# Seven products for eight in the gate, branch and output projections, over one set of PSUM banks

## The chip, the cores and the metric

The kernel runs on one core of a Trainium2 chip. The metric is the device time of one execution in microseconds. Before the change three runs took 2945.49, 2949.14 and 2949.18 us; the median is 2949.14 us.

## What is computed

One layer of a hybrid encoder block over 256 tokens of width 4096, in float32:

```
h    = rms_norm(x)                                    # x: 256 x 4096
proj = h @ w_in                                       # 4096 -> q,k,v,gate, indexer, z,x,B,C,dt, merge logits
y_a  = attention(top 64 keys of an indexer) * silu(gate_a)        # 256 x 2048
y_b  = ssd_mixer(conv, scan) * silu(z), grouped norm              # 256 x 2048
g    = sigmoid(merge logits)                          # two gates of 256 x 4096
out  = (g0 * (y_a @ w_branch_attn) + g1 * (y_b @ w_branch_ssd)) @ w_out
x    = x + rms_norm(out)
```

The change is in the last three lines and in the part of `proj` that gives the merge logits: the gate projection (4096 to 8192 columns), the branch projections (two of 2048 to 4096) and the output projection (4096 to 4096).

## The kernel before

**Three matmuls for one product.** Each float32 operand is split in two parts of a reduced format, high and low: `h = round(a)`, `l = a - h`. A product of a 128 x 128 block of activations (the stationary operand) with a 128 x 512 block of weights is three matmuls into one PSUM bank: low x high, high x low, high x high. ScalarE makes the high part of the weights (L144, L147), VectorE the low part (L145, L148), 1024 elements a row at a time, because two K blocks ("a half") are split together. The activations are split once and stay in SBUF: `xh`, `xl`, then `yah`, `yal` and `ybh`, `ybl` for the branches, `mh`, `ml` for the output projection.

**`gemm`** (L118) does 512 output columns: 32 K blocks (16 in a branch) times two token tiles of 128, so 192 matmuls (96 in a branch), into two banks. The accumulators rotate over two pairs of banks, four more banks are free for other work (`aux_bank`). Weights come in chunks of 1 MB (`raw`, 3 buffers), SyncE issues them. The high and low parts have 3 buffers each (`WBUFS`).

**Side work** runs as generators in a queue `aux`. `step()` advances the first one after each half; `push` adds one. The evacuation of a gemm's two banks is such a generator: it is pushed when the gemm's last matmul has been recorded, and so runs beside the next gemm.

**The stages**: indexer and attention, then the SSD mixer, then a loop over `n` of eight blocks of 512 columns, each with two gate gemms, the attention branch and the SSD branch, then eight output gemms and the final norm. `ev_gate` (L669) takes a sigmoid out of PSUM, `ev_branch` multiplies a branch's PSUM result by it (L678) and GpSimd adds the two branches (L685). The merged block is transposed on TensorE (`transpose4`) and written to DRAM (`mscr`, L699) by GpSimd's DMA queue; `load_merged` (L703 to L712) reads it back near the end and splits it (L709, L710). A scheduler orders the recorded instructions of each engine by their dependencies and their place in the program; each engine then works in order.

Of the kernel before, what the change touches and what calls it, by code (L numbers as in the profile page):

```python
# [22 lines left out]
KC = 4  # L23
HK = 2
WBUFS = 3
EPS = 1e-6
# [4 lines left out]
QSCALE = 128 ** -0.5  # L31
ISCALE = 32 ** -0.5 * 64 ** -0.5
# [6 lines left out]
def fused_block(tc, x, xT, w_qi, w_misc, w_attn, w_ssd, w_gate, w_br, w_out,  # L39
# [13 lines left out]
    dram = root(tc.tile_pool(name="dram", bufs=1, space=bass.MemoryType.DRAM))  # L53

    def aux_bank():
        return paux.tile([P, NW], F32, tag="aux", name="aux")

    xh = big.tile([P, KT, S], F32R, tag="bh", name="xh")
    xl = big.tile([P, KT, S], F32R, tag="bl", name="xl")
# [20 lines left out]
    yraw = [yr.tile([P, 2, S], F32, tag=f"yr{i}", name=f"yraw{i}") for i in range(8)]  # L80

    # ---------------------------------------------------------------- helpers
# [35 lines left out]
    def gemm(chunks, nk, act, evac, prep=None, plan=None, done=None):  # L118
        while len(live) > 1:
            drain(live.popleft())  # L120
        ps = {t: pmain.tile([P, NW], F32, tag=f"acc{t}", name=f"acc{t}") for t in range(2)}
# [44 lines left out]
    def gemm_misc(evac):  # L166
        while len(live) > 1:
            drain(live.popleft())
        ps = pmain.tile([P, S], F32, tag="acc0", name="accm")
        for c in range(KT // KC):  # L170
# [6 lines left out]
            for i in range(KC):  # L177
                k = c * KC + i
                T.matmul(ps, wh[:, i, :], xl[:, k, :], start=(k == 0), stop=False)
                T.matmul(ps, wl[:, i, :], xh[:, k, :], start=False, stop=False)  # L180
                T.matmul(ps, wh[:, i, :], xh[:, k, :], start=False, stop=(k == KT - 1))
# [3 lines left out]
    def xact(k):  # L185
        return xh[:, k, :], xl[:, k, :]

    # ------------------------------------------------------ start: x, its rstd
# [25 lines left out]
    def split_x(k, xk):  # L214
        g = pc[:, PC_GAIN + k:PC_GAIN + k + 1]
        A.activation(xh[:, k, :], xk, AF.Copy, scale=g)
        V.scalar_tensor_tensor(xl[:, k, :], xk, g, xh[:, k, :].bitcast(F32),
                               ALU.mult, ALU.subtract)
# [20 lines left out]
    # ------------------------------------------------------------ attention  # L239
# [26 lines left out]
    def evac_misc(ps):  # L266
# [17 lines left out]
        # softplus(v) = max(v, 0) + log1p(exp(-|v|)), log1p(e) = 2 atanh(e / (2 + e))  # L284
# [93 lines left out]
    def attention_unit(j):  # L378
# [24 lines left out]
        def attend():  # L403
            for t in range(2):
# [46 lines left out]
                for i in range(2):  # L451
                    V.tensor_copy(yraw[2 * j + i][:, :, t * P:(t + 1) * P],
                                  b3[:, 2 * i:2 * i + 2, :])
                yield
# [4 lines left out]
    for j in range(2):  # L459
        gemm([w_qi[j, c] for c in range(8)], KT, xact, qi_rope(j), prep=None if j else prep_x)  # L460
# [3 lines left out]
    for j in range(2, 4):  # L464
        gemm([w_qi[j, c] for c in range(8)], KT, xact, qi_rope(j))
        push(qi_score(j))
    push(topk())
    for j in range(4):
        evs, attend = attention_unit(j)
        for i in range(4):  # L470
            gemm([w_attn[j, i, c] for c in range(8)], KT, xact, evs[i])
        push(attend())

    # ----------------------------------------------------------------- SSD
# [8 lines left out]
    def to_ssd():  # L483
        nonlocal ssdp, ssdp_cm, ybp_cm, ybh, ybl
# [3 lines left out]
        ybp_cm, ybp = open_pool("ybp")  # L488
        ybh = ybp.tile([P, 16, S], F32R, name="ybh")
        ybl = ybp.tile([P, 16, S], F32R, name="ybl")  # L490
        ssdp_cm, ssdp = open_pool("ssdp")

    ssdp = ssdp_cm = ybp_cm = ybh = ybl = None
# [399 lines left out]
```

## Time and profile before

| | |
|---|---|
| time, three runs | 2945.49, 2949.14, 2949.18 us |
| profiled execution, span from first to last instruction | 2946.0 us |
| TensorE busy | 2923.5 us, 13260 matmuls |
| VectorE busy | 1560.6 us |
| ScalarE busy | 1336.8 us |
| GpSimd busy | 198.9 us |
| DMA | 568.09 MB, mean 193 GB/s |

The page gives no other time for the profiled execution than its span, which lies within the three runs. The matmul column counts time in which at least one matmul was in flight; one matmul's row is longer than the distance from its start to the next one's start, since they are pipelined. The same holds for VectorE and ScalarE instructions that stand back to back. Times per stage, distances and waits are in the rows further down.

### The profile page before, as it was taken

The numbers are of one execution on the slowest core, as the hardware profiler recorded it, in microseconds if no ns is written. First come the engines' busy times: TensorE is split into PE (matmuls) and PEld (weight loads), VectorE is DVE, ScalarE is ACT, GpSimd is POOL, SyncE is SP. The second block draws the span as 40 slices with busy tenths as digits, with TensorE's granted clock in tenths as the row PEclk, the third lists the DMA queues.
The fourth block names the chain that finished last, engine by engine and source line by source line (L and its number), as shares of the span: only waits on it lengthen the run. The fifth ranks groups of instructions, "written<-read, shape, count | busy, mean of one in ns | idle before, by whom it ended". The sixth has DMA issues, their size and how long they took to land.

```text
span 2946.0 us, 33033 instructions
## 1 busy us (share of the span) xinstructions
PE 2923.5 (99%) x13260; PEld 2414.2 (82%) x13260; DVE 1560.6 (53%) x1750; ACT 1336.8 (45%) x1548; POOL 198.9 (7%) x150
## 2 busy tenths in 40 slices
PE   9999999999999999999999999999999999999997
PEld 7878888888888888888888888888888888888886
DVE  6677445454454656565655444444444444544445
ACT  6444444444444545555555344444444444444444
POOL 0100000000000103030300000000000000000001
PEclk9999999999999999999999999999999999999998
DMA  9544555545555454545455555555555555675554
GB/s 334 179 168 173 190 181 185 187 171 192 180 186 187 170 184 174 175 168 187 170 186 183 203 194 199 190 203 188 204 195 196 197 192 201 235 269 197 192 194 157
DMA packets 86555, 568.09 MB, mean 193 GB/s; under 512 B 9728, under 2 KB 10496, under 8 KB 20864
## 3 DMA queue, kind: packets, MB, share of 16 engines
q1 hardware_dynamic: 85392, 562.30, 53.7%
q0 software_dynamic: 1008, 3.67, 0.3%
q8 instruction: 104, 1.70, 0.2%
q14 instruction: 51, 0.42, 0.0%
HBM read 558.06 MB, written 7.86 MB: 192 GB/s over the span
## 4 chain that ended last, share of the span: by engine, by line
PE 97%; DMA 1%; DVE 1%; ACT 0%; issue 0%; SPq 0%; ACTq 0%; DVEq 0%
PE acc L156 31%; PE acc L158 31%; PE acc L157 31%; DMA mr<-mscr 1%; PE aux L322 1%; PE aux L581 0%; DMA raw<-w_qi_d 0%; PE aux L350 0%; PE aux L439 0%; PE aux L412 0%; PE aux L571 0%; DVE og L786 0%; PE aux L510 0%; DVE wl L148 0%; PE aux L432 0%
## 5 line engine op out<-in xcount | busy, mean ns | idle before, releaser
L148 DVE TENSOR_TENSOR wl<-raw,wh 128x1024 fp32r<-128x1024 f32 x1011 | 1255.8, 1243 | 1234.8 <-ACT wh L147 1232.6
L147 ACT ACTIVATE wh<-raw 128x1024 fp32r<-128x1024 f32 x1011 | 1071.3, 1060 | 1477.0 <-PE acc L158 1437.6
L156 PE MATMUL acc<-wh,xl 128*128 128x512 f32 x3072 | 1211.4, 395 | 2.4 <-ACT wh L144 1.4
L158 PE MATMUL acc<-wh,xh 128*128 128x512 f32 x3072 | 1197.8, 390 | 0.0
L157 PE MATMUL acc<-wl,xh 128*128 128x512 f32 x3072 | 1197.6, 390 | 0.0
L156 PEld LDWEIGHTS acc<-wh,xl 128*128 128x128 f32 x3072 | 577.1, 188 | 122.7 <-ACT wh L144 2.7
L158 PEld LDWEIGHTS acc<-wh,xh 128*128 128x128 f32 x3072 | 577.0, 188 | 121.5
L157 PEld LDWEIGHTS acc<-wl,xh 128*128 128x128 f32 x3072 | 577.7, 188 | 118.6 <-DVE wl L145 1.5
L157 PE MATMUL acc<-wl,mh 128*128 128x512 f32 x512 | 200.4, 391 | 3.9 <-DVE wl L148 3.9
L158 PE MATMUL acc<-wh,mh 128*128 128x512 f32 x512 | 200.2, 391 | 0.0
L156 PE MATMUL acc<-wh,ml 128*128 128x512 f32 x512 | 200.1, 391 | 0.0
L157 PEld LDWEIGHTS acc<-wl,mh 128*128 128x128 f32 x512 | 96.6, 189 | 24.4 <-DVE wl L148 4.5
L158 PEld LDWEIGHTS acc<-wh,mh 128*128 128x128 f32 x512 | 96.7, 189 | 20.2
L156 PEld LDWEIGHTS acc<-wh,ml 128*128 128x128 f32 x512 | 96.5, 189 | 20.2 <-ACT wh L147 0.2
L157 PE MATMUL acc<-wl,ybh 128*128 128x512 f32 x256 | 99.8, 390 | 0.8 <-DVE wl L148 0.8
L156 PE MATMUL acc<-wh,ybl 128*128 128x512 f32 x256 | 99.7, 390 | 0.2 <-ACT wh L147 0.2
L158 PE MATMUL acc<-wh,ybh 128*128 128x512 f32 x256 | 99.6, 389 | 0.0
L157 PE MATMUL acc<-wl,yah 128*128 128x512 f32 x256 | 99.6, 389 | 0.0
L158 PE MATMUL acc<-wh,yah 128*128 128x512 f32 x256 | 99.6, 389 | 0.0
L156 PE MATMUL acc<-wh,yal 128*128 128x512 f32 x256 | 99.6, 389 | 0.0
L259 POOL TENSOR_TENSOR ro<-m,m 128x512 f32<-128x512 f32 (+1 forms) x26 | 42.4, 1633 | 819.0 <-DVE m L257 810.7
L685 POOL TENSOR_TENSOR m<-sig 128x512 f32<-128x512 f32 x16 | 28.2, 1776 | 885.5 <-DVE sig L678 770.9
(197 smaller groups left out, 1345.7 us busy)
## 6 DMA issues: line engine op xcount, KB each, us to landing
raw<-w_attn_d SPq DMA_DIRECT2D x128, 1024.0 KB, 4.8
raw<-w_gate_d SPq DMA_DIRECT2D x128, 1024.0 KB, 4.8
raw<-w_ssd_d SPq DMA_DIRECT2D x96, 1024.0 KB, 4.8
raw<-w_br_d SPq DMA_DIRECT2D x64, 1024.0 KB, 4.8
raw<-w_out_d SPq DMA_DIRECT2D x64, 1024.0 KB, 4.8
raw<-w_qi_d SPq DMA_DIRECT2D x31, 1024.0 KB, 6.4
xn<-x_d SPq DMA_DIRECT2D x8, 512.0 KB, 5.0
out_d<-og SPq DMA_DIRECT2D x16, 256.0 KB, 2.0
```

Of the source, the lines that this page charges most:

```text
L147: A.activation(wh, rs, AF.Copy)
L148: V.tensor_sub(wl, rs, wh.bitcast(F32))
L156: T.matmul(ps[t], al[:, tk], wh[:, i, :], start=first, stop=False)
L157: T.matmul(ps[t], ah[:, tk], wl[:, i, :], start=False, stop=False)
L158: T.matmul(ps[t], ah[:, tk], wh[:, i, :], start=False, stop=last)
L259: G.tensor_add(ro, m1, m2)
L322: T.transpose(b[:, i * P:(i + 1) * P], src[:, i * P:(i + 1) * P], ident)
L685: G.tensor_add(m, sig[0, t], sig[1, t])
```

## The change

**Two output blocks at a time, in quarters.** `pair_gemm` takes 1024 output columns as two blocks of 512 and K in pairs of blocks. With A = the activations of a K pair (two token tiles by two K blocks) and B = its weights (two K blocks by two column blocks), the step is a 2 x 2 by 2 x 2 block product. A step of kind S makes it with 7 products (Strassen's algorithm in Winograd's form), 21 matmuls of 512 columns, into seven banks 1 to 7, which are combined on evacuation. A step of kind D or R makes it with 8 products, 24 matmuls, into banks 2, 3, 4, 5 (D) or 2, 3, 4, 8 (R), in a form that adds up with the S steps. `kinds` gives the kind of each step: S for K pairs 1, 3, 5, 6, 8, 10, 12 and 14 of sixteen (`SX`, `SM`) in the gate and output projections, for 1, 4, 6, 9, 12, 14 (`SY`, eight pairs a branch) in the branches, and D or R for the rest and for pairs named plain.

**What an S step adds.** VectorE forms `t13` (1024 elements) and two further sums of weights in place in `raw` (512 each), and four splits of weights instead of two, one of them of 512 elements, on ScalarE and VectorE. The activations need sums too (`make_ext`): `ext` holds four sums of a pair for an S step and the two differences for a D step, high and low.

**Evacuation.** The banks 1 to 8 form one set: the next pair begins with the same banks. `early` and `late` copy one bank on ScalarE and make seven or eight adds on VectorE; they are recorded before the next pair, not in a generator.

**Order and places.** First one plain gate gemm of each branch, beside the second of them the sums of x (`ext_x`); then seven gate pairs (`GATES`), whose sigmoids go to DRAM (`sscr`); then four turns of two branch pairs, which read the gates back (`load_sig`); then three output pairs and two plain output gemms. The branch inputs go to DRAM as they are made (`yscr`) and come back through GpSimd's DMA queue (`load_y`, `load_m`) into the space of `base`. The addition of the two branches moves from GpSimd to VectorE (L914). Four buffers instead of three hold the split weights. `aux_bank` has one bank, 8, in the gate and branch pairs.

```diff
-    whp = root(tc.tile_pool(name="whp", bufs=WBUFS))
-    wlp = root(tc.tile_pool(name="wlp", bufs=WBUFS))
-    pmain = root(tc.tile_pool(name="pmain", bufs=2, space=bass.MemoryType.PSUM))
-    paux = root(tc.tile_pool(name="paux", bufs=4, space=bass.MemoryType.PSUM))
+    whp = root(tc.tile_pool(name="whp", bufs=SBUFS))          # SBUFS = 4
+    wlp = root(tc.tile_pool(name="wlp", bufs=SBUFS))
+    pq = root(tc.tile_pool(name="pq", bufs=1, space=bass.MemoryType.PSUM))
...
+    def make_ext(i, a, seven, diff=True):
...
+            V.scalar_tensor_tensor(f[:, 0, :], a21, -1.0, a22, ALU.mult, ALU.subtract)
+            V.tensor_sub(f[:, 2, :], a11, a21)
+            V.scalar_tensor_tensor(f[:, 1, :], f[:, 0, :], -1.0, a11, ALU.mult, ALU.subtract)
+            V.tensor_sub(f[:, 3, :], a12, f[:, 1, :])
+        else:
+            V.tensor_sub(f, a[:, :, 0:P], a[:, :, P:S])
...
+        A.activation(e[:, 0], f, AF.Copy)
+        V.tensor_sub(e[:, 1], f, fbit(e[:, 0]))
+    def make_base(i, a):
+        base[i] = base_tile(i)
+        A.activation(base[i][:, 0], a, AF.Copy)
+        V.tensor_sub(base[i][:, 1], a, fbit(base[i][:, 0]))
...
+        def early():
+            if 1 not in ps or left[1] or dest:
+                return
+            dest.extend(outs())
+            A.activation(dest[0], ps[1], AF.Copy)
+            V.tensor_add(dest[1], ps[6], dest[0])
+            V.tensor_add(dest[2], ps[7], dest[1])
+        def late():
...
+            c11, c12, c21, c22 = dest
+            V.tensor_add(c12, ps[5], c12)
+            V.tensor_add(c22, ps[5], c21)
+            V.tensor_add(c11, ps[2], c11)
+            V.tensor_add(c21, ps[4], c21)
+            V.tensor_add(c12, ps[3], c12)
+            if 8 in ps:
+                V.tensor_add(c22, ps[8], c22)
+        for n, (i, kind) in enumerate(plan):
+            raw = rawp.tile([P, KC, NW], F32, tag="raw", name="raw")
+            nc.sync.dma_start(raw, chunk(i))
...
+            if kind == "S":
+                t13 = tp.tile([P, 2, NW], F32, tag="t13", name="t13")
+                V.tensor_sub(t13, raw[:, 1:3, :], raw[:, 0:1, :].to_broadcast([P, 2, NW]))
+                b11, b22 = split(raw[:, 1:3, :], 2)
+                b21, = split(raw[:, 3:4, :], 1)
+                V.tensor_add(raw[:, 2, :], raw[:, 2, :], t13[:, 0, :])
+                t1, t3 = split(t13, 2)
+                V.tensor_sub(raw[:, 3, :], raw[:, 3, :], raw[:, 2, :])
+                t2, t4 = split(raw[:, 2:4, :], 2)
+                for j, name, w in ((1, "A11", b11), (2, "A12", b21), (3, "S4", b22),
+                                   (5, "S1", t1), (7, "S3", t3), (6, "S2", t2), (4, "A22", t4)):
+                    product(j, i, name, w)
+                early()
...
+        late()
+        live.append(push(evac(dest)))
...
+    def ev_gate(cols):
+        def run(c):
+            for q, o in enumerate(c):
+                t, (n, br) = q // 2, cols[q % 2]
+                A.activation(o, o, AF.Sigmoid, scale=rstd[:, t:t + 1])
+                nc.gpsimd.dma_start(sscr[br, n, t], o)
...
+    def ev_branch(n, br):
+        def run(c):
+            for q, o in enumerate(c):
+                V.tensor_mul(o, o, sig[q // 2, q % 2])
+                if br == 1:
+                    V.tensor_add(o, o, held[q])
...
```

Three places show how the order changes. The first is VectorE between two gemms of the gate stage. Before, only splits of weights (L148) and the gates' products of the branches (L678) stand there:

```order
L678 TENSOR_TENSOR sig<-acc_12670,sig 128x512
L678 TENSOR_TENSOR sig<-acc_12671,sig 128x512
L148 TENSOR_TENSOR wl<-raw,wh 128x1024 x8
L678 TENSOR_TENSOR sig<-acc_12812,sig 128x512
L678 TENSOR_TENSOR sig<-acc_12813,sig 128x512
L148 TENSOR_TENSOR wl<-raw,wh 128x1024 x40
```

Now, at the end of the first gate pair: L732 is the low part in `split`, L763 and L764 the adds of `early`, L776 to L780 those of `late`, L792 `t13`, L795 and L797 the two sums in `raw`. The first step of the next pair is of kind D (two L732), its second of kind S:

```order
L732 TENSOR_TENSOR wl<-raw,wh 128x1024 x3
L763 TENSOR_TENSOR pc<-p_12038,pc 128x512
L732 TENSOR_TENSOR wl<-raw,wh 128x1024
L764 TENSOR_TENSOR pc<-p_12034,pc 128x512
L732 TENSOR_TENSOR wl<-raw,wh 128x1024
L776 TENSOR_TENSOR pc<-p_11971,pc 128x512
L777 TENSOR_TENSOR pc<-p_11971,pc 128x512
L778 TENSOR_TENSOR pc<-p_11975,pc 128x512
L779 TENSOR_TENSOR pc<-p_11979,pc 128x512
L780 TENSOR_TENSOR pc<-p_11983,pc 128x512
L792 TENSOR_TENSOR t_12644<-raw 128x1024
L732 TENSOR_TENSOR wl<-raw,wh 128x1024
```

The two splits of the next pair's first step stand ahead of `late`, those of its second step behind it.

The second place is VectorE at the end of the SSD branch pair of the first turn, where the gate products (L912) and the sum of the branches (L914) follow `late`:

```order
L779 TENSOR_TENSOR pc<-p_16921,pc 128x512
L780 TENSOR_TENSOR pc<-p_16925,pc 128x512
L912 TENSOR_TENSOR pc<-pc,sg 128x512 x2
L914 TENSOR_TENSOR pc<-pc 128x512 x2
L912 TENSOR_TENSOR pc<-pc,sg 128x512 x2
L914 TENSOR_TENSOR pc<-pc 128x512 x2
L792 TENSOR_TENSOR t_17281<-raw 128x1024
L732 TENSOR_TENSOR wl<-raw,wh 128x1024
L732 TENSOR_TENSOR wl<-raw,wh 128x512
L795 TENSOR_TENSOR raw<-raw,t_17281 128x512
```

All eight come before `t13` and the splits of the next pair's second step.

The third is TensorE in a gate pair, where K pair 6 (kind S) follows pair 5 (kind S). The names are banks (`p_12038` is bank 6, `p_11979` bank 4, `p_11971` bank 5), `b_84` and `b_85` the activations of pairs 6 and 7:

```order
L756 MATMUL p_12038<-wh,ext 128x512
L756 MATMUL p_11979<-wh,b_84 128x512
L756 MATMUL p_11971<-wh,b_85 128x512
L756 MATMUL p_11975<-wh,b_85 128x512
L756 MATMUL p_11983<-wh,ext 128x512
L756 MATMUL p_12038<-wl,ext 128x512
L756 MATMUL p_12038<-wh,ext 128x512
```

Five matmuls that need only high parts stand ahead of the one that needs the low part of pair 6's last split; elsewhere a product's three matmuls stand together.

## Rows read from the trace of the kernel before

**Rows 1.** The page: span, busy time of each engine.
```profile
span 2946.0 us, 33033 instructions
PE 2923.5 (99%) x13260; PEld 2414.2 (82%) x13260; DVE 1560.6 (53%) x1750; ACT 1336.8 (45%) x1548; POOL 198.9 (7%) x150
```

**Rows 2.** The chain that ended last, shares of the span by engine and line.
```profile
PE 97%; DMA 1%; DVE 1%; ACT 0%; issue 0%; SPq 0%; ACTq 0%; DVEq 0%
```

**Rows 3.** Busy time by stretch: us, each engine (instructions), granted clock, DMA share, GB/s.
```profile
1633.00:1764.60 131.60, 131.60 (x586) 108.96 (x585) 61.70 (x54) 54.41 (x54) 4.25 (x3) 1.00 0.56 200
2578.00:2665.00 87.00, 87.00 (x390) 72.03 (x389) 42.44 (x39) 37.54 (x40) 3.52 (x2) 1.00 0.72 260
2930.00:2946.00 16.00, 3.57 (x9) 2.27 (x7) 8.45 (x14) 2.22 (x5) 5.21 (x3) 0.61 0.46 171
```

**Rows 4.** Timeline of TensorE: start, duration; first and last of 57 matmuls.
```profile
1959.67 0.39 PE L158 MATMUL acc<-wh,xh 128*128 128x512 f32 x1
...
1972.36 0.39 PE L157 MATMUL acc<-wl,xh 128*128 128x512 f32 x1
```

**Rows 5.** Groups by line and shape: count, busy us, mean ns, idle before.
```profile
L148 DVE TENSOR_TENSOR wl<-raw,wh 128x1024 fp32r<-128x1024 f32 x1011 | 1255.8, 1243 | 1234.8 <-ACT wh L147 1232.6
L145 DVE TENSOR_TENSOR wl<-raw,wh 128x512 fp32r<-128x512 f32 x32 | 20.5, 688 | 7.5 <-ACT wh L144 7.5
L575 DVE TENSOR_TENSOR mm<-mm,cbm 128x512 f32<-128x512 f32 x16 | 17.6, 1100 | 5.3 <-ACT mm L574 5.3
L584 DVE TENSOR_TENSOR yv<-yv,aux 128x512 f32<-128x512 f32 x8 | 5.5, 687 | 11.2 <-PE aux L581 11.2
L362 DVE SCALAR_TENSOR_TENSOR score<-rl,wi,score 128x128 f32<-128x128 f32 x31 | 10.9, 350 | 1.2
L669 ACT ACTIVATE sig<-acc,rstd 128x512 f32<-128x512 f32 x32 | 21.8, 689 | 15.4 <-PE acc L158 15.1 <-issue 0.3
```

**Rows 6.** Timeline of VectorE, instructions back to back.
```profile
81.85 1.22 DVE L148 TENSOR_TENSOR wl<-raw,wh 128x1024 fp32r<-128x1024 f32 x1
82.99 0.68 DVE L254 TENSOR_TENSOR m<-acc,tab 128x512 f32<-128x512 f32 x1
83.59 0.41 DVE L255 TENSOR_TENSOR m<-acc,tab 128x256 f32<-128x256 f32 x1
83.92 0.41 DVE L257 TENSOR_TENSOR m<-acc,tab 128x256 f32<-128x256 f32 x1
```

**Rows 7.** Timeline of ScalarE, instructions back to back.
```profile
2551.55 1.04 ACT L147 ACTIVATE wh<-raw 128x1024 fp32r<-128x1024 f32 x1
2552.50 0.61 ACT L709 ACTIVATE mh<-mr 128x512 fp32r<-128x512 f32 x1
2553.02 1.04 ACT L147 ACTIVATE wh<-raw 128x1024 fp32r<-128x1024 f32 x1
```

**Rows 8.** Timeline of TensorE, ScalarE and VectorE about one split.
```profile
2000.47 0.39 PE L158 MATMUL acc<-wh,xh 128*128 128x512 f32 x1
2000.90 1.06 ACT L147 ACTIVATE wh<-raw 128x1024 fp32r<-128x1024 f32 x1 [1.66 <-PE acc L158]
2001.99 1.23 DVE L148 TENSOR_TENSOR wl<-raw,wh 128x1024 fp32r<-128x1024 f32 x1 [1.50 <-ACT wh L147]
```

**Rows 9.** Waits: engine and line, what released it, us, times, longest.
```profile
ACT wh L147 <- PE acc L158: 1437.6, 877, 4.0
ACT mh L709 <- DMA mr<-mscr: 12.8, 5, 4.0
PE acc L157 <- DVE wl L148: 4.6, 2, 3.9
```

**Rows 10.** DMA issues: queue, count, KB each, median us to landing.
```profile
raw<-w_gate_d SPq DMA_DIRECT2D x128, 1024.0 KB, 4.8
mscr<-mT POOLq DMA_DIRECT2D x7, 512.0 KB, 4.1
mr<-mscr SPq DMA_DIRECT2D x14, 256.0 KB, 4.2
```

More of the change, by code (lines that the diff above doesn't have):

```diff
@@ L120, in gemm @@
             drain(live.popleft())
-        ps = {t: pmain.tile([P, NW], F32, tag=f"acc{t}", name=f"acc{t}") for t in range(2)}
+        accs.rotate(-1)
+        ps = {t: bank(accs[0][t]) for t in range(2)}
         plan = plan or [(h, (0, 1)) for h in range(nk // HK)]
@@ L459, in fused_block @@
     for j in range(2):
[L460 removed]
+        gemm([w_qi[j, c] for c in range(8)], KT, act, qi_rope(j), prep=None if j else prep_x)
     gemm_misc(evac_misc)
@@ L464, in fused_block @@
     for j in range(2, 4):
-        gemm([w_qi[j, c] for c in range(8)], KT, xact, qi_rope(j))
+        gemm([w_qi[j, c] for c in range(8)], KT, act, qi_rope(j))
         push(qi_score(j))
@@ L470, in fused_block @@
         for i in range(4):
-            gemm([w_attn[j, i, c] for c in range(8)], KT, xact, evs[i])
+            gemm([w_attn[j, i, c] for c in range(8)], KT, act, evs[i])
         push(attend())
@@ L665, in ev_gate, with set_tags @@
-    def ev_gate(br):
+    ext = {}
+    ext_tag = {}
+    extb = exts = tp = None
+    kind_of = dict.fromkeys(range(16), "x")
+    def set_tags(seven):
+        for half in range(2):
+            here = range(8 * half, 8 * half + 8)
+            big_ = [f"eb{i}" for i in SX if i in here]
+            small = [f"es{i}" for i in here if i not in SX]
+            for i in here:
+                if i in seven:
+                    ext_tag[i] = big_.pop(0)
+            for i in here:
+                if i not in seven:
+                    ext_tag[i] = (small or big_).pop(0)
@@ new lines, in forms_from, with kinds, yr4 @@
+    def forms_from(what, load, seven, pairs, diff=True):
+        a = load(pairs[0])
+        for i in pairs:
+            ahead = load(i + 1) if i + 1 in pairs else None
+            make_base(i, a)
+            make_ext(i, a, seven, diff)
+            kind_of[i] = what
+            a = ahead
+            yield
+    def kinds(seven, pairs, plain=()):
+        return [(i, "D" if i not in seven else "R" if i in plain else "S") for i in pairs]
+    def yr4(first):
+        return [yr.tile([P, NW], F32, tag=f"yr{first + i}", name="pc") for i in range(4)]
@@ new lines, in run, with start_m @@
+            yield
+        return run
+    held = []
+    for n in range(0, 8, 2):
+        for br in range(2):
+            pairs = range(8 * br, 8 * br + 8)
+            plain = pairs if (n, br) in ((0, 0), (6, 1)) else ()
+            plan = kinds(SY, pairs, plain)
+            hooks = {5: lambda: load_sig(n, br)}
+            if (n, br) == (0, 0):
+                hooks[0] = lambda: push(forms_from("y", load_y, SY, range(8, 16)))
+            if (n, br) == (6, 1):
+                def start_m():
+                    set_tags(SM)
+                    push(forms_from("m", load_m, SM, range(8), False))
+                hooks[0] = start_m
+            pair_gemm("y", lambda i: w_br[n // 2, br, i % 8], plan, lambda: yr4(4 * br),
+                      ev_branch(n, br), hooks)
@@ new lines, in fused_block, with done_branch @@
+    for n in range(0, 6, 2):
+        if n == 0:
+            order = (0, 2, 4, 7, 1, 9, 3, 11, 5, 13, 6, 15, 8, 12, 10, 14)
+            plain = (8, 12, 10, 14)
+        else:
+            order, plain = range(16), ()
+        plan = [(i, "R" if k == "D" else k) for i, k in kinds(SM, order, plain)]
+        def done_branch():
+            while len(aux) > 1:
+                step()
+            brp_cm.__exit__(None, None, None)
+            exts_cm.__exit__(None, None, None)
+            open_og()
+        pair_gemm("m", lambda i: w_out2[n // 2, i], plan, ogs(n), ev_pair(n),
+                  {10: done_branch} if n == 0 else {}, 1 if n else 2)
```

376 lines of the change are left out of this document (243 added, 133 removed).

## The prediction

> **What bounds the kernel now.** The page comes first: TensorE is busy 2923.5 of 2946.0 us, VectorE 1560.6, ScalarE 1336.8 [rows 1]. The chain that ended last is TensorE for 97% of the span [rows 2]. The table by stretch shows the same inside the stages that change: in one turn of the gate and branch loop TensorE is busy 131.60 of 131.60 us, VectorE 61.70 and ScalarE 54.41; in an output stretch VectorE 42.44 of 87.00; the granted clock is 1.00, the 2.4 GHz level [rows 3]. From the first to the last of 57 matmuls in a row pass 12.69 us, so one costs 12.69 / 56 = 0.2266 us [rows 4]. The waits say who sets the pace: ScalarE's splits wait 1437.6 us in total for TensorE to free a buffer, TensorE's second matmuls wait 4.6 us for VectorE's low part [rows 9]. So a matmul left out is worth 0.2266 us as long as the splits keep up, and VectorE has half its time free to do so.
>
> **What goes.** The three stages hold 3072 matmuls in the gates (16 gemms of 192), 1536 in the branches (16 of 96) and 1536 in the output (8 of 192). Now a gate or output pair has 8 S steps of 21 and 8 of 24, 360 for 384. Gates: 2 plain gemms, six such pairs and one with 4 S steps (372): 384 + 2160 + 372 = 2916. Branches: six pairs with 3 S steps (183) and two without (192): 1482. Output: 372 + 2 x 360 + 384 = 1476. Left out are 156 + 54 + 60 = 270, at 0.2266 us: **-61.2 us**. The count rules out that the change doesn't do what it says.
>
> **What VectorE gets.** Rows of 1024 elements last 1.24 us, of 512 0.69, also out of PSUM [rows 5]; but back to back a 1024 starts 1.14 us before its successor (81.85 to 82.99), a 512 0.60, a 256 0.33 [rows 6]. An S step has four of 1024 and three of 512: 4 x 1.14 + 3 x 0.60 = 6.4 us against 21 x 0.2266 = 4.76 on TensorE. A D or R step has 2.3 against 5.44. A gate pair is 8 x 8.7 + 8 adds x 0.60 = 74 us of VectorE against 81.6 of TensorE. ScalarE, 0.95 us for 1024 back to back and 0.52 for 512 [rows 7], has 3.4 us in an S step and is never the fuller one. It fits on average, so the loss lies where the order bunches the work. No row shows `t13`, whose second operand is broadcast; bounds are 1.14 us and, by the 512 with a broadcast operand that stood beside GpSimd work (1.10) [rows 5], 2.2. I take 1.14, since GpSimd computes nothing in these stages now. An added wait can't be below nothing.
>
> The Trainium skill (VectorE: DVE Perf Modes, The DRAIN you can't avoid) says that the next Vector operation starts only when the pipe of the one before is empty; another section of that page lets it start earlier when nothing holds it. The first would make every row count in full, and is a rival below. The starts 1.14 us apart under rows of 1.22 us [rows 6] speak against it.
>
> **S behind S.** Pair 6 follows pair 5. Count from pair 5's first matmul. A buffer frees when the last reader's row ends (2000.47 + 0.39, ScalarE at 2000.90, VectorE 1.09 later) [rows 8]. Pair 6's first buffer frees after nine matmuls, 8 x 0.2266 + 0.39 = 2.2 us; ScalarE to 3.3, VectorE's low part to 4.6, next low part 5.1, the sum 5.7, low parts of `t13` 6.9, the second sum 7.5. Only then can ScalarE split the last two, to 8.6; VectorE makes the `t13` of pair 8 meanwhile and their low part to 9.9. TensorE wants the first at 4.76 + 15 x 0.2266 = 8.2 and waits 0.4. The order then puts four matmuls that need high parts alone ahead of the low part; three of them need pair 7's split (to 9.6): another 0.5. So 1.0 us, nine times (seven gate, two output pairs): **+9**. From both sides: 0 if VectorE were ahead by a step, 1.7 without the reordering.
>
> **End of a gate pair.** Count from step 14; step 15 ends at 10.2. VectorE: low parts to 5.6, two adds and the next pair's two splits to 9.1, then `late`: bank 5 free at 10.4, bank 3's add at 12.2. TensorE wants bank 5 at 10.2: 0.2 us. ScalarE's sigmoids (0.69 each) [rows 5] then stand ahead of the split of b21: the second needs bank 3's add, four end at 14.2, and through b21, sums and splits the last low part of the next S step comes at 20.2, half a microsecond after TensorE wants it. 0.75 x 7 = **+5**. The three output ends, whose squares and gain products stand in the same place, go by the same working to 0.5, 2.0 and 1.5: **+4**.
>
> The Trainium skill (Perfetto Trace Analysis, Matmuls) asks that matmul groups rotate through PSUM banks so that one's evacuation runs beside the next. The change gives that up: one set of eight. By the rule alone the adds would stand bare at each of 18 ends, which is rival E; the working above leaves 0.2 us of them bare. No row of before shows either, since its accumulators rotate.
>
> **End of a branch pair.** Behind `late` come four products with the gates, at the SSD branch four sums too, all ahead of `t13`: 8 x 0.60 = 4.9 us. The first low part of the next S step then comes at 19.4; TensorE wants it at 16.1. It fills part with first matmuls and eight transposes, but those share one bank with a ScalarE copy between. I get 3.4 us at three ends, 2 us at two (four products), 0.5 at the three others: **+16**. Bounds 6 (all filled) and 27 (none: 5.4, 3.3).
>
> **Sums of activations and DRAM.** `ext_x` takes 8 x 2.4 + 8 x 1.3 = 30 us of VectorE, mostly beside a plain gemm, whose 16 low parts at 1.14 leave 43.5 - 18.3 = 25: about 3 us late. A 128-wide dependent operation is 0.35 [rows 5]. 28 loads come back through DRAM where 14 did. Those took 4.2 us to land, the writes 4.1 [rows 10], and held ScalarE for 12.8 us over five waits [rows 9]; with two buffers a pair of loads costs 6 to 7 us against 5.44 of TensorE. The buffers of split weights hide most of it; I take 5. Together **+8**, bounds 2 and 20. The sigmoids' stores and the weights at 1 MB per 4.76 us and 4.8 us to land [rows 10] I cost at nothing: three buffers hide them; without that cover an S step would lose some 0.5 us.
>
> **Sum.** -61.2 + 9 + 5 + 4 + 16 + 8 = -19 us, against 2946. The three runs hold the span, and their median is 3 above it: 2949 - 19 = **2930 us**. The stages before the gates, the last two gemms and the last 16 us don't change.
>
> **Rivals.**
> *The splits run ahead (B).* Four buffers instead of three and the scheduler's order cover half of the 42 us of waits: 2949 - 61 + 21 = 2909. For it: TensorE waited 4.6 us in all for low parts [rows 9], beside side work as dense. Against: the last split of an S step can't start before the sum that the step before holds up.
> *VectorE becomes the bound (C), slower.* If instructions cost their rows, an S step is 4 x 1.24 + 3 x 0.69 = 7.0 us, D 2.5, a gate pair 76 + 5.5 = 81.6, as much as TensorE's 81.6. Nothing is caught up then: 2 us at each S behind S (18), 2.2 at ten gate and output ends (22), 5.4 and 3.3 at branch ends (25), 12 for the sums: 77 - 61 = +16, 2965 us. It decides from a VectorE load of about 95% in a gate pair. For it: rows 6 show only neighbours that don't depend on each other, and the two sums in `raw` do. Against: the distances in rows 6.
> *The gain is just eaten (D).* Branch ends and DRAM loads at their upper bounds, 11 + 12 more: +4, 2953; any mixture ends within 6 us of before.
> *The adds stand bare (E).* If the next pair's first matmul waited for the last add at each of the 18 ends, 4.8 us each, all 86 us would come on top of the other waits: 3015. For it: all eight banks are in use. Against: the order puts bank 5, which is finished 4 us early, first on both sides.
> The clock is a risk in all: in the last 16 us, with TensorE busy 3.57, 0.61 was granted [rows 3]. The waits here are 1 to 3 us in 40, so I expect 1.00.
>
> **Chances.** Forecast (2918 to 2943) 0.43, B 0.20, C 0.22, D 0.13, E 0.02. A difference under 0.2%, 6 us, can't be told from none. Faster than 2943: the forecast with some spill, and B: 0.57; within: 0.16; slower, C, E and a part of D: 0.27. The range takes in B's centre and C's: 2904 to 2967. The likeliest case alone is 2918 to 2943.
>
> **What would show it.** Matmuls 12990 in number, 0.227 us apart. A gate pair 83 to 84.5 us for 87 before, VectorE 0.88 to 0.93 busy there; waits of TensorE on L732 in pair 6 (about 1 us) and in the second step after a gate pair. A branch pair 43.5 to 46 us, no shorter than before, with 2 to 3.5 us of waiting in its second step. An output pair about 84. Wrong would be: gaps in steps where D follows S, VectorE's distances near its rows' lengths, bank waits above 1 us at the first matmul of a pair, or ScalarE held by `fr` for more than 20 us with TensorE idle behind it.

## The result and the profile after

The changed kernel takes 2915.31 us (median of four runs, 2913.67 to 2916.41) against 2948.10 for the kernel before: ratio 0.9889, 95% interval 0.9875 to 0.9903, so 1.0 to 1.25% faster, 33 us by the medians. 2930 had been predicted; 2915 lies in the range (2904 to 2967), 3 us under the forecast's own one.

The page of the profiled execution after, answering to [rows 1]:

```profile
span 2914.0 us, 33808 instructions
PE 2875.6 (99%) x12990; PEld 2356.7 (81%) x12990; DVE 2039.2 (70%) x2490; ACT 1499.5 (51%) x1799; POOL 210.4 (7%) x209
```

270 matmuls are gone, as counted, and VectorE has 479 us more to do. The span falls by 32.0 us, 29 less than 270 x 0.2266 = 61.2. The table by stretch shows where it went (columns as in [rows 3]): the second and the sixth gate pair, the last gate pair, the branch pairs behind the first SSD end and behind the next attention end, and two output pairs.

```profile
1693.66:1776.73 83.07, 82.50 (x362) 67.16 (x360) 74.83 (x80) 48.36 (x54) 2.18 (x4) 1.00 0.61 221
2027.14:2109.51 82.37, 82.16 (x362) 67.27 (x360) 74.85 (x80) 48.36 (x54) 2.17 (x4) 1.00 0.59 217
2109.51:2198.60 89.09, 86.08 (x373) 69.36 (x372) 79.42 (x115) 55.39 (x73) 9.86 (x18) 1.00 0.65 239
...
2284.88:2331.25 46.37, 44.44 (x201) 35.84 (x199) 40.88 (x51) 23.48 (x28) 2.19 (x4) 1.00 0.64 238
2331.25:2374.75 43.50, 42.54 (x185) 34.04 (x183) 38.05 (x43) 21.55 (x24) 0.00 (x0) 1.00 0.58 218
2642.31:2725.17 82.86, 82.44 (x362) 67.12 (x360) 74.56 (x81) 48.30 (x56) 0.00 (x0) 1.00 0.55 203
2725.17:2810.58 85.41, 83.67 (x361) 66.91 (x360) 77.48 (x85) 48.34 (x58) 0.00 (x0) 1.00 0.68 250
```

A window runs from a pair's first matmul to the next pair's. What it has beyond its matmuls at 0.2266 us is waiting: 360 make 81.6, so the second gate pair waits 1.5 us, the sixth 0.8; 372 make 84.3, so the last gate pair waits 4.8; 183 make 41.5, so the two branch pairs wait 4.9 and 2.0. VectorE is busy 74.8 us in a gate pair, where 74 had been worked out. The columns of busy time alone would mislead: TensorE shows 82.50 of 83.07, since rows of 0.39 to 0.50 us stand 0.2266 us apart and a part of a late start lies under the row before it.

Which waits these are, by the list of waits (us in total, times, longest):

```profile
ACT wh L731 <- PE p L756: 335.1, 254, 3.7
ACT wh L731 <- DVE raw L797: 76.4, 37, 3.0
...
ACT b L715 <- DMA fr<-yscr: 18.5, 10, 2.9
DVE t L792 <- DMA raw<-w_gate_d: 14.7, 15, 2.6
...
PEld p L756 <- DVE wl L732: 16.5, 30, 1.5
```

In [rows 9] the splits waited for TensorE. Now 76 us of their waits, in 37 places, end with the second sum of weights (L797): there VectorE sets the pace. And `t13` (L792) waits for the weights themselves, a wait that the prediction put at nothing.

### The profile page after: what moved, and what is told of

It reads as the page before. It is cut to its first block, busy times and chain, and to the rows that moved or that the text cites. A ratio compares the mean times of both kernels' runs of the same rounds, so it can differ in the third digit from the quotient of the medians.

```text
span 2914.0 us, 33808 instructions
## 1 busy us (share of the span) xinstructions
PE 2875.6 (99%) x12990; PEld 2356.7 (81%) x12990; DVE 2039.2 (70%) x2490; ACT 1499.5 (51%) x1799; POOL 210.4 (7%) x209
## 5 line engine op out<-in xcount | busy, mean ns | idle before, releaser
L169 DVE TENSOR_TENSOR wl<-raw,wh 128x1024 fp32r<-128x1024 f32 x563 | 699.0, 1243 | 597.5 <-ACT wh L168 595.3
L168 ACT ACTIVATE wh<-raw 128x1024 fp32r<-128x1024 f32 x563 | 596.5, 1060 | 795.6 <-PE p L179 754.6
L177 PE MATMUL p<-wh,b 128*128 128x512 f32 x2304 | 911.1, 396 | 1.4 <-ACT wh L165 1.4
L178 PE MATMUL p<-wl,b 128*128 128x512 f32 x2304 | 898.7, 390 | 3.5 <-DVE wl L169 3.3
L179 PE MATMUL p<-wh,b 128*128 128x512 f32 x2304 | 898.4, 390 | 0.0
L756 PE MATMUL p<-wh,b 128*128 128x512 f32 x2300 | 757.2, 391 | 4.5 <-ACT wh L731 3.2
L731 ACT ACTIVATE wh<-raw 128x1024 fp32r<-128x1024 f32 (+1 forms) x538 | 510.5, 984 | 312.9 <-PE p L756 214.4
L732 DVE TENSOR_TENSOR wl<-raw,wh 128x1024 fp32r<-128x1024 f32 (+1 forms) x538 | 584.3, 1130 | 82.5 <-ACT wh L731 79.5
L756 PEld LDWEIGHTS p<-wh,b 128*128 128x128 f32 x2300 | 430.6, 188 | 101.3 <-ACT wh L731 11.2
L178 PEld LDWEIGHTS p<-wl,b 128*128 128x128 f32 x2304 | 433.3, 188 | 93.2 <-DVE wl L169 4.4
L177 PEld LDWEIGHTS p<-wh,b 128*128 128x128 f32 x2304 | 432.8, 188 | 92.3 <-ACT wh L165 3.0
L179 PEld LDWEIGHTS p<-wh,b 128*128 128x128 f32 x2304 | 432.6, 188 | 91.5
L756 PE MATMUL p<-wl,b 128*128 128x512 f32 x1150 | 448.5, 390 | 2.2 <-DVE wl L732 2.1
L756 PE MATMUL p<-wh,ext 128*128 128x512 f32 x1104 | 387.1, 391 | 4.8 <-ACT wh L731 4.8
L756 PEld LDWEIGHTS p<-wl,b 128*128 128x128 f32 x1150 | 215.9, 188 | 49.3 <-DVE wl L732 4.5
L756 PE MATMUL p<-wl,ext 128*128 128x512 f32 x552 | 217.2, 394 | 4.4 <-DVE wl L732 4.4
L792 DVE TENSOR_TENSOR t<-raw 128x1024 f32<-128x1024 f32 x90 | 109.9, 1221 | 28.7 <-DMA raw<-w_gate_d 14.7
L732 DVE TENSOR_TENSOR wl<-t,wh 128x1024 fp32r<-128x1024 f32 x90 | 109.9, 1222 | 16.5 <-ACT wh L731 15.7
```

The source lines that it names most:

```text
L168: A.activation(wh, rs, AF.Copy)
L169: V.tensor_sub(wl, rs, wh.bitcast(F32))
L177: T.matmul(ps[t], al[:, tk], wh[:, i, :], start=first, stop=False)
L178: T.matmul(ps[t], ah[:, tk], wl[:, i, :], start=False, stop=False)
L179: T.matmul(ps[t], ah[:, tk], wh[:, i, :], start=False, stop=last)
L731: A.activation(h, src, AF.Copy)
```

## The experiments

Each is timed against the kernel before on the same chip (2947 to 2948 us). The interval of a ratio is about 4 us wide to either side, so totals less than some 5 us apart are not told apart here; the stretches of the traces decide then.

**All steps plain.** What do the S steps save, and what does the layout cost?

```
plan = kinds(SX, range(16), range(16))     # the branches and the output likewise
```

(where no product goes to bank 5, as then in the output pairs, the evacuation is four copies on ScalarE without adds).

> Every step of the gate, branch and output pairs is plain (8 products), the layout (pairs over one bank set, gates first, results through DRAM, adds on evacuation) stays, and the sums of activations are still made. Theory A (the forecast): the 270 matmuls pay 0.2266 us each, and most of the about 28 us of waits that the changed kernel shows belong to S steps (their split chain behind S steps, at branch and output ends, weights held longer). All plain gives back 61 us and drops some 18 to 24 of the waits: 2915 + 61 - 21 = 2955 us, 2950 to 2962. Rival L (the waits belong to the layout, S steps cost nothing): 2915 + 61 = 2976, 2970 or more. Rival H (a part of the gain comes from the layout, not from the products left out): under 2946, the time before.

Measured 2957.42 us, ratio 1.0032 (1.0020 to 1.0044). In the stretch of the second gate pair 384 matmuls stand without a gap:

```profile
1696.72:1783.76 87.04, 87.04 (x385) 72.10 (x384) 40.34 (x34) 37.86 (x40) 2.17 (x5) 1.00 0.59 211
```

The other six gate pairs take 87.04 us too, so the waits in the gate pairs are the S steps' own: the seven pairs take 587.7 us with them and 609.3 without, 21.6 saved of the 35.3 that 156 matmuls are worth. The totals would give 42 of 61 for all S steps, and 9.5 us as the cost of the layout, but they show neither: the plain branch pairs have waits that the changed kernel doesn't have. The worst is the last attention pair, 47.71 us in the changed kernel:

```profile
2487.55:2542.82 55.27, 48.49 (x205) 38.93 (x204) 33.27 (x48) 24.86 (x32) 3.84 (x7) 0.94 0.67 233
```

There VectorE waits up to 6.7 us for merged blocks from DRAM (L701). Besides, the transposes share bank 8 with the plain steps (plain branches, below). The six branch pairs from the first SSD end on take 286.4 us for 271.0, where the products account for 10. So theory A holds for the gate pairs; that the total comes near its 2955 is in part chance.

**Three buffers for the splits**, as the kernel before had.

```diff
-SBUFS = 4
+SBUFS = 3
```

> Three buffers instead of four for the high and for the low parts in every gemm, nothing else. Rival B's reason (the fourth buffer lets the splits run ahead and covers part of the waits): with three the low parts come up to one split, 1.1 us, later wherever VectorE is behind, at the 9 S behind S, the 10 gate and output ends and the 5 branch ends, 10 to 25 us more: 2925 to 2940. Theory A (the last split of an S step can't start before the sum that the step before holds up, whatever the number of buffers): 2913 to 2919.

Measured 2978.03 us, ratio 1.0104 (1.0088 to 1.0119): 63 us slower than with four, and slower than before the change. The second gate pair, and TensorE's wait for low parts, which in the changed kernel ends its weight loads' idle time 30 times and here 168 times:

```profile
1699.18:1787.18 88.00, 86.36 (x361) 65.87 (x360) 76.22 (x80) 49.12 (x54) 2.17 (x4) 1.00 0.57 209
```

```profile
PEld p L756 <- DVE wl L732: 71.3, 168, 1.4
```

A gate pair of 360 matmuls now takes longer than one of 384. By start-to-start distances 2.4 us are lost where S follows S, and 0.3 to 0.6 us in every other S step too. My expectation was wrong in both of its readings: the fourth buffer is no reserve for a few places but what lets an S step keep up.

**A fifth split buffer in the gates.**

```diff
+        more = gate_pools and spn[0] % 5 == 0
-        h = whp.tile([P, n, NW], F32R, tag="wh", name="wh")
+        h = (gate_pools[0] if more else whp).tile([P, n, NW], F32R, tag="wh", name="wh")
```

(the low part likewise).

> In the gate stage every fifth split of weights goes into one more buffer for the high and one for the low part, so five are in use instead of four. Theory B (what is left at S behind S is a matter of buffers, as three instead of four made it 2.4 instead of 0.65 us there and 0.5 after every other S step): S behind S goes to under 0.2 us, gate pairs to 81.7 to 82.2 us; the waits for late weights stay: 2915 - 4 = 2911, 2908 to 2912. Theory A as predicted (the chain of sums on VectorE holds the last split, whatever the buffers): 0.6 us stay in each pair, 2913 to 2917.

Measured 2914.49 us, ratio 0.9890 (0.9876 to 0.9903): no gain in all, but the trace is clear. The third gate pair and the last:

```profile
1774.70:1856.30 81.60, 81.60 (x362) 67.59 (x361) 74.12 (x80) 48.66 (x54) 2.16 (x4) 1.00 0.59 215
2101.42:2194.56 93.14, 86.70 (x373) 69.13 (x372) 78.45 (x114) 53.58 (x72) 9.84 (x18) 1.00 0.65 234
```

360 matmuls in 81.60 us, no wait at all; the six pairs take 81.6 to 82.6. So the wait where S follows S is a matter of buffers, and the argument that the chain of sums holds the last split whatever the buffers falls. Of the 7 us that the six pairs won in the profiled execution 4 go at the end of the last gate pair (93.14 for 89.09), where VectorE's adds stand behind low parts that are late because ScalarE and VectorE wait for `fr` through DRAM. The next pair's first matmul waits for an add:

```profile
2194.56 0.47 PE L759 MATMUL p<-wh,b 128*128 128x512 f32 x1 [3.74 <-DVE pc L780]
```

That is rival E's wait (an add that stands bare), at one end only.

**A fourth weights buffer in the gates.**

```diff
-            raw = rawp.tile([P, KC, NW], F32, tag="raw", name="raw")
+            rawn[0] += 1
+            raw = (rawx if what == "x" and rawn[0] % 4 == 0 else rawp).tile(
+                [P, KC, NW], F32, tag="raw", name="raw")
```

> In the seven gate pairs every fourth weights tile comes from one more buffer of 1 MB, so four chunks can be under way instead of three. Theory W (an S step holds its weights until its last split, so the next chunk's transfer starts late; t13 waits 0.4 us for the DMA even where S follows S, and 2 us in single steps): the 0.6 to 0.9 us of each pair's sixth and seventh K pair shrink to under 0.3 and the single waits of 0.7 to 1.4 us (four in all) go: 2915 - 4 - 3 = 2908, 2906 to 2910. Theory A as predicted (the wait where S follows S is the chain of sums and splits on VectorE and ScalarE): only the single waits go, 2911 to 2914.

Measured 2914.78 us, ratio 0.9885 (0.9871 to 0.9898): no gain in all. The fourth gate pair, which took 84.01 before this edit, and the first branch pair, which took 44.80:

```profile
1856.64:1938.80 82.16, 81.95 (x362) 67.44 (x360) 76.02 (x80) 48.74 (x54) 2.16 (x4) 1.00 0.59 217
...
2192.70:2241.78 49.08, 45.86 (x193) 37.01 (x193) 29.04 (x35) 23.65 (x29) 2.17 (x4) 0.97 0.58 207
```

The single waits of 0.7 to 1.4 us are gone from the second to the fifth pair (the sixth has a new one of 0.7), and of the 14.7 us that `t13` waited for gate weights 3.0 are left; 0.6 us where S follows S stay. So late weights are the single waits and not the wait of S behind S. The gain is lost again at the same place as with the fifth buffer, but not by need: the first combined form has this buffer too and doesn't lose there (below).

**Four S behind S in a gate pair instead of one.**

```diff
-SX = (1, 3, 5, 6, 8, 10, 12, 14)
+SX = (1, 2, 5, 6, 9, 10, 13, 14)
```

> In the gate stage S steps stand at K pairs 1, 2, 5, 6, 9, 10, 13, 14: as many products and as much work of every engine, but four S behind S in a pair instead of one (19 more in all). Theory A (the chain of splits and sums behind an S step costs 0.65 us each time, as measured where S follows S, and two D steps behind make it up): 2915 + 19 x 0.65 = 2927, 2923 to 2932. As the prediction sized it, 1.0 each: 2934. Rival V (VectorE's mean load alone decides, the order doesn't): 2913 to 2917.

Measured 2932.97 us, ratio 0.9946 (0.9933 to 0.9958): 18 us more than the order of the change, with the same work. The third gate pair:

```profile
1781.64:1867.41 85.77, 84.06 (x362) 66.65 (x360) 75.34 (x80) 47.98 (x54) 2.16 (x4) 1.00 0.58 209
```

4.2 us of waits: 0.5 to 0.6 at each of three S behind S, as theory A had it, but 0.7 and 1.8 at pairs 1 and 2, which meet the adds of the pair before. The mean load of VectorE (rival V) does not decide; order does. The total is just above theory A's range because of pairs 1 and 2; that it fits the 1.0 us of my prediction is chance.

**One more VectorE instruction in an S step.**

```diff
+                if what == "x":
+                    V.tensor_sub(t13[:, 0, :], raw[:, 1, :], raw[:, 0, :])
```

> In each of the 52 S steps of the gate pairs VectorE makes half of t13 a second time, one more instruction of 512 elements (0.60 us back to back), 4.8 us a pair: its load in a pair goes from 74.8 to 79.6 of about 83 us, 0.96. Theory A (the price shows only on the chain behind S steps and at the ends): S behind S 0.6 to 1.2 us more, the second step of a pair up to 1 more, seven pairs: 2920 to 2930. Rival C's condition (from a load of 95% VectorE catches nothing up and bounds the pair): 2 more at S behind S, 2.2 at each end and more between, 2940 and above. If it is all hidden: 2914 to 2917.

Measured 2933.63 us, ratio 0.9950 (0.9938 to 0.9963). The second gate pair and the fifth:

```profile
1695.53:1780.58 85.05, 83.86 (x362) 66.75 (x360) 79.39 (x88) 47.79 (x54) 2.21 (x5) 1.00 0.60 217
1951.22:2040.95 89.73, 86.53 (x361) 68.76 (x360) 79.36 (x88) 47.99 (x54) 2.17 (x5) 0.96 0.54 199
```

4.8 us more of VectorE cost 2 us in an ordinary pair: 1.2 where S follows S and 0.9 in the second step, with small ones between and at the end. Theory A named the places and sized them low: its range ends at 2930, and most of what lies above is the fifth pair, which has a wait of its own (last section). VectorE at 79.4 of 85 is not yet the bound, as rival C needs, but the order makes 40% of what is added visible.

**Plain branches.**

```diff
-            plain = pairs if (n, br) in ((0, 0), (6, 1)) else ()
+            plain = pairs
```

> Only the branch pairs are plain; gates and output keep their S steps. 54 matmuls come back, 12.2 us. Theory A: the S steps of the branches gain nothing, since at five of their ends the second step waits 2.0 (four products) or about 2.7 us (products, sums, transposes) and the last step of one pair 1: 2915 + 12.2 - 13 = 2914, 2910 to 2918. Rival (the waits at the ends come from the evacuation and the transposes, whatever the steps are): 2927 or more.

Measured 2923.24 us, ratio 0.9915 (0.9902 to 0.9929), 8 us more. The waits in the second step are gone, but plain pairs accumulate in bank 8, which the transposes use too, and those are now late. The same two branch pairs as above:

```profile
2283.83:2328.81 44.98, 44.98 (x206) 37.01 (x204) 25.15 (x26) 20.26 (x22) 0.54 (x1) 1.00 0.63 223
2328.81:2377.38 48.57, 45.88 (x198) 37.42 (x196) 25.20 (x28) 19.77 (x23) 1.64 (x3) 0.96 0.61 216
```

Neither expectation is met. The edit changes two things at once, so this says only that these S steps are better than plain steps with that bank; inconclusive on what they are worth.

**Gate products of the branches later.**

```diff
         def run(c):
+            for _ in range(3):
+                yield
```

> The gate products and the sums of the branches start three turns later in the side-work queue, so they stand behind the second step's splits on VectorE instead of ahead of t13; nothing else is added or removed. Theory A (these four or eight instructions, 2.4 or 4.8 us, are the wait in the second step): the waits of 2.0 us at two ends and 2.7 at three go, 8 to 12 us: 2904, 2902 to 2908. Rival M (the backlog only moves: VectorE is 0.88 to 0.92 busy in these pairs, and a later step is late by as much): 2913 to 2917. Rival T (the wait belongs to the transposes, which share one bank with a ScalarE copy): only the two ends without transposes gain, 4 us: 2911.

Measured 2910.48 us, ratio 0.9873 (0.9859 to 0.9886). The three branch pairs from the first SSD end on:

```profile
2281.26:2325.42 44.16, 43.99 (x200) 35.56 (x199) 40.40 (x51) 23.42 (x28) 2.18 (x4) 1.00 0.68 248
2325.42:2367.13 41.71, 41.71 (x185) 34.30 (x184) 38.11 (x43) 21.50 (x24) 0.00 (x0) 1.00 0.61 229
2367.13:2414.33 47.20, 45.32 (x201) 37.05 (x199) 39.94 (x47) 23.38 (x28) 1.07 (x2) 0.96 0.61 223
```

The attention end is now almost free (41.71 for 43.50), so the four products were its wait. Of the SSD ends one gains (44.16 for 46.37) and one loses (47.20 for 46.38): there ScalarE's split waits for weights:

```profile
2382.47 1.58 ACT L731 ACTIVATE wh<-raw 128x1024 fp32r<-128x1024 f32 x2 [3.77 <-DMA raw<-w_br_d]
```

The last branch pair, plain, loses 5 us more (48.61 for 43.52), with low parts late behind sums that wait for merged blocks from DRAM. So theory A holds for the cause of the wait. Something later is late instead, as rival M has it, but by weights and merged blocks and not by VectorE's load.

**The attention branch's first S step as its third, its own products later.**

```diff
-SY = (1, 4, 6, 9, 12, 14)
+SY = (2, 4, 6, 9, 12, 14)
+            for _ in range(3 if br == 0 else 0):
+                yield
```

> The attention branch's first S step is its third (K pairs 2, 4, 6 instead of 1, 4, 6), so the products, sums and transposes of the pair before meet two D steps; the attention branch's own products start three turns later in the side-work queue. Counts of all instructions are the same. Theory A: the second-step waits go, 2.0 us at two ends and about 2.8 (beside transposes) at three: 2915 - 12 = 2903, 2901 to 2907. Rival T (the transposes' own chain through one bank and ScalarE stays): 2909 to 2912. Rival M (VectorE is late at a later step by as much): 2913 to 2917.

Measured 2907.12 us, ratio 0.9861 (0.9848 to 0.9875). The same three pairs:

```profile
2280.24:2330.73 50.49, 46.79 (x200) 37.45 (x199) 40.83 (x51) 23.60 (x28) 2.18 (x4) 0.93 0.60 218
2330.73:2372.25 41.52, 41.52 (x185) 34.35 (x183) 37.70 (x43) 21.54 (x24) 0.00 (x0) 1.00 0.61 228
2372.25:2416.36 44.11, 43.66 (x201) 35.83 (x200) 40.13 (x47) 23.83 (x28) 1.07 (x2) 1.00 0.65 238
```

Both kinds of end work as theory A says: 41.52, and 44.11, which is 41.5 of products, 2.2 of transposes and 0.4. The first has a new wait, which is no end's: VectorE works in order, and the scheduler put the sums of a merged block there, before that block was back from DRAM:

```profile
2306.30 0.29 DVE L701 SCALAR_TENSOR_TENSOR frm<-fr 128x128 f32<-128x128 f32 x1 [5.35 <-DMA fr<-mscr]
```

**Combined.** The fourth weights buffer, the edit before this and the same delay for the squares and gain products of two output pairs; then, in its last form, the fifth split buffer instead of the weights buffer, half the pace for the sums of y in the last gate pair, and a buffer that keeps the early read of the merged block back:

```diff
+                if (n, br) == (4, 0) and t == 1:
+                    sig[t, b] = tp.tile([P, NW], F32, tag="fr", bufs=2, name="fr")
```

> The fourth weights buffer in the gates, the moved S step of the attention branch, the later products of the attention branch and of the first two output pairs' squares and gain products, together. Sum of what the single edits showed: gates 4 us of single waits, branch ends 10, output ends 1 to 2, less 0 to 5 where the scheduler places loads of activations anew: 2915 - 13 = 2902, 2898 to 2908. If they share one reserve of VectorE and one gives back what the other takes: 2908 to 2915.

> The fifth split buffer in the gates, the moved S step and the later products and squares of the run before; besides, the sums of y are made at half the pace in the last gate pair, and the first merged block is read back only after the fourth branch pair, through a buffer that a gate block holds until then. Theory B: gate pairs 81.6 to 82.1 us for 82.2 to 83 (-3 us against the combined version before), no wait of 4 us in the third branch pair (-5), and in the last gate pair at most 2 us beside the matmuls: 2901 - 8 = 2893, 2889 to 2898. If the loads through DRAM still hold ScalarE in the last gate pair, as they did with the fifth buffer alone (8.8 us): 2898 to 2905.

Measured 2901.48 us, ratio 0.9849 (0.9836 to 0.9863), and 2897.73 us, ratio 0.9832 (0.9818 to 0.9845). The last form is faster than both kernels, by 17.6 us against the change; the two forms are too close to rank. The last gate pair and the two pairs where the first form had lost 4 and 1 us:

```profile
2102.49:2191.29 88.80, 84.84 (x374) 69.43 (x372) 78.61 (x114) 53.96 (x72) 9.87 (x18) 1.00 0.68 245
2278.03:2323.07 45.04, 44.04 (x200) 35.76 (x199) 40.13 (x47) 23.82 (x28) 1.07 (x2) 1.00 0.63 233
2364.61:2408.70 44.09, 43.63 (x200) 35.83 (x199) 40.13 (x47) 23.83 (x28) 1.07 (x2) 1.00 0.64 237
```

The end of the last gate pair still waits 4.5 us, where the second expectation had at most 2, and its 2893 was 5 too low. The first form, with the fourth weights buffer instead, waited 1.5 us there:

```profile
2103.78:2189.53 85.75, 85.18 (x374) 69.51 (x373) 79.01 (x114) 54.87 (x72) 9.83 (x18) 1.00 0.68 249
```

The sums of y, which VectorE makes beside this pair, differ between the runs in kind and pace. What sets the wait at this end is not shown.

## Why the prediction was right, and where it was off

The direction and the mechanism were right: the products left out pay their 0.2266 us each, and what is lost again is waits at the places that were named. The sum was 13 us too careful. Its terms, against what the trace after shows beyond the matmuls:

| term | predicted | measured | from |
|---|---|---|---|
| 270 matmuls | -61.2 | -61.2 | 0.2266 each |
| S behind S | +9 | +6.5 | seven gate pairs 0.6 to 0.9, output 0.6 and 1.0 |
| ends of gate pairs | +5 | 0 | no gap in a second step of the second to the seventh |
| output ends | +4 | +2.3 | 1.4 in the last pair, 0.9 at the plain gemm |
| branch ends | +16 | +12.3 | second steps: 3 x 2.75 beside the transposes, 2 x 2.0 |
| sums and DRAM | +8 | +7.2 | 0.5, 4.1, 1.3 and 1.3 about the plain gemm, the last gate pair, the first branch pair, the last attention pair |
| weights | 0 | +5.5 | single waits: gates 3.7; output 1.8, where the end before may have a share |
| last two gemms | 0 | -4.2 | below; -3.3 with the 0.9 that stands at the output ends |

The sum of the right column is -31.6, the spans' difference -32.0. (Eight transposes cost 1.1 us in [rows 3]: 131.60 less 576 x 0.2266; sixteen 2.2.)

The waits come to 34 us, where the forecast had 42 and rival B 21, so the forecast's account is the nearer one; in the total, 2915, B's 2909 is nearer than 2930. 4 us of that are the last two gemms', which no theory had; without them the time would lie inside the forecast's own range. And the terms miss both ways: five are 14 us too high together, the one put at nothing is 5.5 too low. That the total lies as near as it does is in part luck. (The prediction has 27 us as the upper bound of the branch ends in one place and 25 in another; 5.4 at three ends and 3.3 at two give 23.)

**S behind S.** The place is right and the size is 6.5 of the 9 us that were worked out. VectorE and ScalarE, then TensorE, at pairs 5 and 6 of the second gate pair:

```profile
1725.81 0.68 DVE L797 TENSOR_TENSOR raw<-raw 128x512 f32<-128x512 f32 x1
1726.61 4.62 ACT L731 ACTIVATE wh<-raw 128x1024 fp32r<-128x1024 f32 x5 [2.27 <-PE p L756]
```

```profile
1728.06 0.40 PE L756 MATMUL p<-wh,b 128*128 128x512 f32 x1
1728.67 0.73 PE L756 MATMUL p<-wh,b 128*128 128x512 f32 x2 [0.21 <-ACT wh L731]
```

1728.06 to 1728.67 is 0.61 for one matmul, 0.38 lost there; the rest lies in the matmuls around it. By the order shown ahead of the prediction, 1728.06 is bank 4's matmul and 1728.67 the first that needs pair 7's split. So this is the second of the two waits in the working (0.5); of the first (0.4, for pair 6's last split) 0.05 is left, and TensorE waits for ScalarE's high part, not for L732, which had been named as the sign. The reason that I gave against rival B failed: ScalarE starts these splits at 1726.61, 0.1 us after the sum that was said to hold them (L797, to 1726.49), but the profile has it wait for TensorE to free a buffer, and with five buffers the wait goes. B had the right lever, and pulled the other way it makes the change a loss. The working had four buffers in it, but not how steep their number is: a gate pair takes 88.0 us with three, 82.4 to 84.0 with four, 81.6 to 82.6 with five.

**Ends of gate pairs.** The order shown ahead of the prediction ran as it stands, but quicker. VectorE, then ScalarE, at the end of the first gate pair (1693.66):

```profile
1694.38 0.68 DVE L780 TENSOR_TENSOR pc<-p,pc 128x512 f32<-128x512 f32 x1
```

```profile
1694.15 2.55 ACT L851 ACTIVATE pc<-pc,rstd 128x512 f32<-128x512 f32 x4
```

Bank 3's add (L780) ends at 1695.06, 1.4 us after the pair, where 2.0 had been worked out; the four sigmoids end at 1696.70, 3.0 us after it instead of 4.0. By the same working, what came half a microsecond late then comes half a microsecond early. No first step of a gate pair waits for an add, so rival E did not happen there. It did in part at one end, the one behind the last gate pair, where the first matmul of the first branch pair comes 1.3 us late:

```profile
2198.60 0.47 PE L756 MATMUL p<-wh,b 128*128 128x512 f32 x1 [1.19 <-ACT b L715]
```

The profile names ScalarE's split of y, which ends at the same moment; what this matmul needs is bank 5, whose second add (L777) runs from 2197.78 to 2198.46, late behind sums of y and low parts. The prediction had named a bank wait above 1 us as a sign of being wrong; it is counted under sums and DRAM. Another of its signs, `fr` holding ScalarE for more than 20 us, came too: it was 26 (18.5 for y, 7.8 for merged blocks), of which TensorE lost some 7.

**Branch ends.** Mechanism as predicted; VectorE and TensorE at the first SSD end, where eight products and sums (L912, L914) precede `t13`:

```profile
2286.19 1.28 DVE L912 TENSOR_TENSOR pc<-pc,sg 128x512 f32<-128x512 f32 x2
...
2289.80 1.28 DVE L914 TENSOR_TENSOR pc<-pc 128x512 f32<-128x512 f32 x2
2291.01 1.22 DVE L792 TENSOR_TENSOR t<-raw 128x1024 f32<-128x1024 f32 x1
```

```profile
2292.30 0.66 PE L346 MATMUL p<-ct,pc 128*128 128x128 f32 x4 [0.69 <-ACT mT L349]
2293.43 0.50 PE L756 MATMUL p<-wh,ext 128*128 128x512 f32 x1 [0.47 <-ACT wh L731]
```

2.75 us there for 3.4 predicted, 2.0 for 2 at the attention ends, nothing for 0.5 at three others. Two edits that let the splits pass these products take the wait away.

**VectorE's price and rival C.** 0.60 us between 512s and 1.14 between 1024s held throughout, `t13` included, so the condition of C was not met. Neighbours that depend on each other are dearer, L795 and L797 in the second gate pair:

```profile
1752.26 0.68 DVE L795 TENSOR_TENSOR raw<-raw,t 128x512 f32<-128x512 f32 x1
1752.98 0.69 DVE L797 TENSOR_TENSOR raw<-raw 128x512 f32<-128x512 f32 x1
```

0.72 us from start to start, the whole row and 0.04 more. The Trainium skill (VectorE: DVE Perf Modes, The DRAIN you can't avoid) has the next operation wait until the pipe is empty, and start earlier when it is not held. The trace shows the full row for this dependent pair, and 0.60 us for the independent neighbours. The order mostly puts a low part between two dependent sums, so it costs little.

**Weights.** The term put at nothing, "three buffers hide them", failed. An S step holds `raw` until its last split, so the transfer two or three steps on starts late; 0.7 to 1.4 us in four gate pairs, gone with a fourth buffer.

**The last two gemms**, said not to change, went from 93.21 us (first to last matmul) to 89.90. TensorE near the end, before and after:

```profile
2928.51 0.79 PE L157 MATMUL acc<-wl,mh 128*128 128x512 f32 x1 [3.88 <-DVE wl L148]
```

```profile
2899.44 0.50 PE L178 MATMUL p<-wl,b 128*128 128x512 f32 x1 [1.95 <-DVE wl L169]
```

The wait is half as long, and behind the longer one the clock had fallen to the 1.2 GHz level (0.61 over the last 16 us, [rows 3]), which it does not now. The last low part stands ahead of the final addition (L1039) instead of behind it (L781). The run with three buffers has the new order too, and says how much is the buffer's: from its first matmul to the end of its last, the last gemm takes 50.3 us before, 48.2 in the new order with three buffers, 45.9 with four. So each has about half, as far as two kernels can be compared that differ elsewhere.

## What to carry to other kernels

Work moved from a full engine to a half-empty one pays by its order and by the buffers between the engines, not by the mean load: count how many buffers the burst of a step needs, and what its longest-held input keeps from being loaded. Adds on evacuation over a single set of banks can be free if the bank finished first is used first and VectorE comes to them in time; side work that follows them should wait until the next splits are through. When a local edit shows in its own stretch but not in the total, look for the next place where something waits in order for a transfer.

## What the runs showed of the hardware

A wait of TensorE can cost more than itself. In the fifth gate pair of the run with one more VectorE instruction, TensorE and then the granted clock by stretch:

```profile
1964.08 0.79 PE L756 MATMUL p<-wl,ext 128*128 128x512 f32 x1 [2.01 <-DVE wl L732]
1964.67 0.63 PE L756 MATMUL p<-wh,ext 128*128 128x512 f32 x1
1965.10 0.63 PE L756 MATMUL p<-wl,b 128*128 128x512 f32 x1
```

```profile
1966.00:1970.00 4.00, 4.00 (x11) 3.12 (x10) 3.24 (x5) 0.63 (x1) 0.00 (x0) 0.50 1.00 420
```

TensorE had idled 0.17, 0.21 and then 2.01 us, one soon after the other; behind that the clock is at 0.50, the 1.2 GHz level, and matmuls start 0.43 us apart instead of 0.227. The 1.95 us near the end of the changed kernel (L178, above) left the clock at 1.00; behind the 3.74 us of the run with a fifth split buffer (L780, above) it was 0.57 from 2194.5 to 2198.
